# One decoder layer on one core: the RWKV inversion's blocks transposed on chip, and the S5 products rearranged

## The chip, the cores and the metric

The kernel runs on one core of one Trainium2 chip. A core has five engines with a queue each: TensorE (PE, matrix products; its weight loads are listed apart as PEld), VectorE (DVE), ScalarE (ACT), GpSimd (POOL) and SyncE (SP, which here only issues transfers). Results of matrix products lie in PSUM banks, everything else on chip in SBUF with 128 partitions; DRAM is reached by transfers (DMA). The metric is the device time of the program in microseconds (us).

## The reference

One layer of a decoder over 1024 tokens of width 1024, all in float32. Two branches, RWKV-7 and S5, are computed from one input projection, gated, merged and projected; then comes an MLP with a short convolution.

```python
h = rms_norm(x, norm_mix_pre)
p_rwkv, u_s5, gates = split(h @ w_in)               # 1792, 512 and 2048 columns

# RWKV-7, 8 heads of 64: a recurrent state S (64x64) per head
S = S * w_t + (S @ a_t) b_t^T + v_t k_t^T           # a_t = -kk, b_t = kk * a
y_t = S @ r_t
bonus = sum(r * k * r_k) * v                        # added to the normalised y

# S5, 32 groups of 16 channels with 64 complex states each
bu = einsum('gpc,blgc->blgp', b_bar, u)             # complex b_bar
s_t = a_bar * s_{t-1} + bu_t                        # complex, diagonal
y = real(einsum('gcp,blgp->blgc', c, s)) + d * u

x = x + rms_norm((g_rwkv * o_rwkv + g_s5 * o_s5) @ w_out)
x = x + rms_norm(conv_ffn(rms_norm(x)))
```

The RWKV state isn't stepped token by token: the tokens go in chunks of 64, and inside a chunk the recurrence becomes a triangular system, whose unit triangular matrices have to be inverted. The S5 recurrence is worked in steps of 8 tokens (an impulse response of 8 taps, called `kpad` and spread into the Toeplitz tile `toep`, does what lies inside a step; a scan over 128 steps does the rest), with real and imaginary parts on the two halves of the partitions. A rotation of the frame by the angle of a_bar (`cs` and `sn`, cosine and sine) leaves a scan with a real factor `ph`.

## The kernel before

**How the order comes about.** PE's order is the order in which the program is written. A function `drive()` writes it: several lanes (generators) yield how many us of PE work they have issued and how long to wait before they go on; a virtual clock `now` counts what was issued, and while all lanes wait, `background()` takes the next piece from a list of fill work. The constants T_... are these waits. So a longer wait does not stop PE: it puts more fill between two steps of a lane. The other engines' instructions are put in order by the tile framework, with priorities (`high_priority`), and wait in their queues by semaphores.

**The phases.** At first x is read and normalised. Phase 1 runs `s5_lane` and `tab_lane` over four batches of 8 groups; the fill is the input projection (`mix_in`), whose products are the three matmuls of L172 to L174 (a float32 product as three products of split high and low parts, `hh`, `hl`, `wh`, `wl`) and whose evictions are L1083 (ACT) and L1084, L1086 (DVE). Weights arrive in `wf` by SP and are split by ACT (L156) and DVE (L157). Phase 2 opens new pools of SBUF and PSUM (`rk`, `evb`, `psy`) and runs four lanes: two `prep_lane`s (pairs of heads g = 0 and 1), `chain_lane` and `out_lane`, for two halves of the tokens (th = 0 and 1). Its fill is first the gates (`gate_tiles`, evicted by ACT in L1158) and then the merge of the half that is done (`merge`, with DVE's L1203, L1249, L232). After that come the rest of the merge, the output projection and the MLP.

**S5 in a batch.** `s5_tables` makes the tables: `wT` by 8 transposes (L546) that two ACT instructions put out, with a third slice that is the negated real part; `ca` and a copy of it with halves exchanged and one negated, `cb`; `kpad` by 8 products of 16 columns each (L555), all on the same 16 output partitions, evicted by one ACT copy. `s5_batch` then makes two products B for each group (L599: `p1` and `p2`, the second with the parts exchanged), rotates them (DVE, L602 to L604), scans (L605), rotates back (L606, L607), and after a wait T_SCAN of 13 us makes three products C for each group (L612 to L614: `toep`·u, `ca`·z, `cb`·rot), which ACT evicts (L615) and SP stores in the DRAM tensor `YU` (L616).

**The RWKV inversion.** `rwkv_front` ends with the grams (L716), masked by DVE into the tile `gr` (L720). `rwkv_inv` inverts the 32x32 diagonal blocks of all heads and chunks of a half at once: 128 partitions stand for (pair of heads, block, row), and the other index pairs lie along a partition. To get there the blocks go through DRAM: 8 transfers of POOL from `gr` to `md` (L729) and one from `md` into `mt` (L777). After a wait T_MT of 8 us and the transposes of `rwkv_nat`, DVE does 30 steps of two instructions (L789, L791; the copy L784 starts them), which update the inverse `x` in place. Then `x` goes back: one transfer into `xd` (L793) and 8 into the blocks of `gr` (L798). After a wait T_INV (th 0, 43 us) or T_INV2 (th 1, 50 us) `rwkv_level` joins the 32x32 blocks to 64x64 ones, with four transposes by DVE (L812) and products of 32x32 tiles (L822).

For the bonus, `rwkv_setup` scales a block matrix of ones by r_k on DVE (L627).

Of the kernel before, what the change touches and what calls it, by code (L numbers as in the profile page):

```python
# [66 lines left out]
class Kern:  # L67
# [425 lines left out]
    def s5_tables(self, b, d):  # L493
# [37 lines left out]
        cb = self.s5p.tile([128, 8, 9, 16], F32, tag="cb", name=self.nm("cb"), bufs=2)  # L531
# [22 lines left out]
        for g in range(8):  # L554
            mm(ps[0:16, g], bb[:, g, :], ca[:, g, 0:8, :], start=g % 4 == 0, stop=True, skip_group_check=True)  # L555
        A.copy(kpad[:, :, 7:15, :], ps[0:16].rearrange("p g (j c) -> p g j c", c=16))
# [24 lines left out]
        d.update(ca=ca, cb=cb, cs=cs, sn=sn, toep=toep, wT=wT, ph=ph)  # L581
        yield 1.8, T_TRIG

    def s5_batch(self, b, d, ys):
# [4 lines left out]
        ca, cb, cs, sn, toep, wT, ph = (d[n] for n in ("ca", "cb", "cs", "sn", "toep", "wT", "ph"))  # L589
# [6 lines left out]
        p1, p2 = (self.chk().rearrange("p (g n) -> p g n", n=128) for _ in range(2))  # L596
        for p, o in ((p1, 0), (p2, 1)):
            for g in range(8):
                mm(p[:, g], wT[:, g, o:o + 2, :], u8[:, g, :], start=g % 4 == 0, stop=True, skip_group_check=True)  # L599
        r2 = self.t4(shape=(128, 8, 128))  # L600
        lead, turn = (slice(None), slice(None), slice(0, 127)), rot[:, :, 1:128]
        V.tensor_tensor(turn, p1[lead], cs[lead], ALU.mult)  # L602
        V.tensor_tensor(r2[lead], p2[lead], sn[lead], ALU.mult)
        V.tensor_tensor(turn, turn, r2[lead], ALU.add)  # L604
        V.tensor_tensor_scan(*(t.rearrange("p g n -> p (g n)") for t in (z, ph, rot)), 0.0, ALU.mult, ALU.add)  # L605
        V.tensor_tensor(rot, z, sn, ALU.mult)  # L606
        V.tensor_tensor(z, z, cs, ALU.mult)  # L607
        y8 = self.t4(shape=(128, 8, 128))
        yield 3.6, T_SCAN
        ps = self.chk().rearrange("p (g n) -> p g n", n=128)  # L610
        for g in range(8):
            mm(ps[:, g], toep[:, g], u8[:, g, :], start=g % 4 == 0, stop=False, skip_group_check=True)  # L612
            mm(ps[:, g], ca[:, g, 1:9, :], z[:, g, :], start=False, stop=False, skip_group_check=True)
            mm(ps[:, g], cb[:, g, 1:9, :], rot[:, g, :], start=False, stop=True, skip_group_check=True)  # L614
        A.copy(y8, ps)  # L615
        nc.sync.dma_start(ys.rearrange("j c g n -> (j c) g n"), y8)  # L616
        yield 5.4, 0

# [1387 lines left out]
```

## Time and profile before

| | |
|---|---|
| time, median of 3 runs | 1477.7 us (1474.89, 1477.7, 1479.7) |
| profiled execution, its time | 1475.75 us |
| its span, first to last instruction | 1474.0 us |
| mean granted clock of TensorE | 0.987 |
| ACT busy | 729.6 us (50% of the span) |
| POOL busy | 58.9 us (4%) |
| DMA | 206.26 MB, 140 GB/s mean |

The span is that of one profiled execution; its time has 1.75 us around the span. In the rows a group reads: line, engine, operation, the tile written and the tiles read, shapes, count, then busy time and mean duration, then the engine's idle time just before, and what ended it. Matmul records overlap, since they are pipelined: what a matmul costs is the distance from one start to the next, not its record's length. A float32 matmul of 128 columns shows as two records.

### The profile page before, as it was taken

What the parts mean: (1) busy time and instruction counts of PE and PEld (TensorE: products, weight loads), DVE (VectorE), ACT (ScalarE), POOL (GpSimd) and SP (SyncE); (2) the same over time, 40 slices, a digit from 0 to 9 for tenths busy, and PEclk for the clock granted to TensorE, in tenths of its full rate; (3) what the DMA queues carried; (4) which work ended last, traced back from release to release, by engine and by line L of the source; (5) the groups of instructions that cost most, each with busy time, mean ns of one, the idle gap of its engine ahead of it and who ended that gap; (6) DMA issues with size and microseconds to landing.
All of it is one profiled execution on the core that took longest, in us unless ns stands there. A gap on an engine that the chain in (4) does not pass through costs nothing. (4 is left out here: it accounts for less than half of the span.)

```text
span 1474.0 us, 24155 instructions
## 1 busy us (share of the span) xinstructions
PE 1420.3 (96%) x9284; PEld 1161.8 (79%) x9284; DVE 1072.4 (73%) x1761; ACT 729.6 (50%) x1167; POOL 58.9 (4%) x116
## 2 busy tenths in 40 slices
PE   7999999999999999899999999999999999999996
PEld 5778888788877777677788877888888887888775
DVE  8977775665425859657698798777777777697677
ACT  7677654443334653634455454444444544444441
POOL 0000000011100110100000000000000000000001
PEclk9999999999999999899999999999999999999998
DMA  6453433643511575633474543222222227934723
GB/s 219 116 194 120 134 96 88 206 123 117 171 62 63 170 238 164 187 124 108 142 223 145 192 136 112 82 86 86 86 86 86 73 71 256 341 123 140 243 75 114
DMA packets 121284, 206.26 MB, mean 140 GB/s; under 512 B 29248, under 2 KB 35520, under 8 KB 121168
## 3 DMA queue, kind: packets, MB, share of 16 engines
q1 hardware_dynamic: 113296, 182.43, 39.3%
q0 software_dynamic: 6144, 19.99, 4.0%
q10 hardware_dynamic: 1728, 2.29, 0.4%
q8 instruction: 73, 1.20, 0.3%
q14 instruction: 43, 0.35, 0.1%
HBM read 150.14 MB, written 52.43 MB: 137 GB/s over the span
## 5 line engine op out<-in xcount | busy, mean ns | idle before, releaser
L172 PE MATMUL gm<-hh,wh 128*128 128x512 f32 x672 | 276.4, 411 | 9.4 <-DVE ev L1203 4.1
L173 PE MATMUL gm<-hl,wh 128*128 128x512 f32 x672 | 264.8, 394 | 0.1
L174 PE MATMUL gm<-hh,wl 128*128 128x512 f32 x672 | 264.5, 394 | 0.0
L156 ACT CAST wh<-wf 128x512 fp32r<-128x512 f32 x171 | 105.7, 619 | 167.4 <-PE gm L173 99.5
L157 DVE TENSOR_TENSOR wl<-wf,wh 128x512 fp32r<-128x512 f32 x171 | 117.3, 688 | 75.7 <-ACT wh L156 75.1
L172 PEld LDWEIGHTS gm<-hh,wh 128*128 128x128 f32 x672 | 127.5, 190 | 42.1 <-issue 6.0
L174 PEld LDWEIGHTS gm<-hh,wl 128*128 128x128 f32 x672 | 127.6, 190 | 28.0
L173 PEld LDWEIGHTS gm<-hl,wh 128*128 128x128 f32 x672 | 127.8, 190 | 24.7 <-issue 1.0
L1626 PE MATMUL d<-xl,wh 128*128 128x512 f32 x308 | 120.2, 390 | 2.8 <-DVE xl L227 2.8
L1625 PE MATMUL d<-xh,wh 128*128 128x512 f32 x308 | 120.1, 390 | 2.1 <-ACT xh L226 2.1
L1627 PE MATMUL d<-xh,wl 128*128 128x512 f32 x308 | 119.9, 389 | 0.0
L1451 PE MATMUL rp<-t,h 128*128 128x512 f32 x216 | 84.4, 391 | 1.9 <-ACT p L1465 1.9
L1453 PE MATMUL rp<-t,l 128*128 128x512 f32 x216 | 84.2, 390 | 0.5 <-DVE l L227 0.5
L1452 PE MATMUL rp<-t,h 128*128 128x512 f32 x216 | 84.1, 389 | 0.0
L1626 PEld LDWEIGHTS d<-xl,wh 128*128 128x128 f32 x308 | 57.8, 188 | 15.6 <-DVE xl L227 3.9
L1625 PEld LDWEIGHTS d<-xh,wh 128*128 128x128 f32 x308 | 57.8, 188 | 14.5 <-ACT xh L226 2.4
L1627 PEld LDWEIGHTS d<-xh,wl 128*128 128x128 f32 x308 | 57.8, 188 | 12.0
L226 ACT CAST h<-r 128x1024 fp32r<-128x1024 f32 x34 | 35.8, 1054 | 61.1 <-PE rp L1452 29.6
L227 DVE TENSOR_TENSOR l<-r,h 128x1024 fp32r<-128x1024 f32 x34 | 41.7, 1225 | 29.3 <-ACT h L226 27.7
L1472 DVE SCALAR_TENSOR_TENSOR y<-zv,vecs,y 128x1023 f32<-128x1023 f32 (+1 forms) x36 | 46.1, 1281 | 8.5 <-ACT y L1470 8.5
L1451 PEld LDWEIGHTS rp<-t,h 128*128 128x128 f32 x216 | 40.5, 188 | 11.3 <-ACT p L1465 2.7
L1465 ACT COPY p<-rp 128x512 f32<-128x512 f32 x54 | 31.0, 574 | 36.6 <-PE rp L1453 36.6
(459 smaller groups left out, 3163.7 us busy)
## 6 DMA issues: line engine op xcount, KB each, us to landing
r<-in_w_up_dram SPq DMA_DIRECT2D x36, 512.0 KB, 3.7
wf<-in_w_in_dram SPq DMA_DIRECT2D x62, 256.0 KB, 3.1
st<-in_w_down_dram SPq DMA_DIRECT2D x55, 256.0 KB, 4.1
st<-ACT SPq DMA_DIRECT2D x44, 256.0 KB, 4.3
wf<-in_w_up_dram SPq DMA_DIRECT2D x36, 256.0 KB, 2.9
ACT<-y POOLq DMA_DIRECT2D x18, 512.0 KB, 2.9
GT<-ev SPq DMA_DIRECT2D x32, 256.0 KB, 2.5
wf<-in_w_br_dram SPq DMA_DIRECT2D x32, 256.0 KB, 2.9
```

The source lines that it names most:

```text
L156: nc.scalar.copy(h[:, :n], f[:, :n])
L157: nc.vector.tensor_tensor(l[:, :n], f[:, :n], h[:, :n].bitcast(F32), ALU.subtract)
L172: mm(ps, a, xh[k], start=k == 0, stop=False)
L173: mm(ps, a, xl[k], start=False, stop=False)
L174: mm(ps, b, xh[k], start=False, stop=k == n - 1)
L1451: mm(ps, wh[:, c], xh, start=first and k == 0, stop=False, skip_group_check=True)
L1452: mm(ps, wh[:, c], xl, start=False, stop=False, skip_group_check=True)
L1453: mm(ps, wl[:, c], xh, start=False, stop=k == 3, skip_group_check=True)
L1472: V.scalar_tensor_tensor(y[:, lag:], z[:, 0:1024 - lag], self.vec(nme, i), y[:, lag:], ALU.mult, ALU.add)
L1625: mm(ps, wh[:, c], xh[:, x], start=start, stop=False, skip_group_check=True)
L1626: mm(ps, wh[:, c], xl[:, x], start=False, stop=False, skip_group_check=True)
L1627: mm(ps, wl[:, c], xh[:, x], start=False, stop=stop, skip_group_check=True)
```

## The change

- **S5, B.** Only `p1` is multiplied. The second product is replaced by two ACT instructions that copy the halves of `p1`, exchanged and one negated, into `r2`; DVE's product with `sn` is then made in place. `wT` holds 128 columns for each group and is evicted by one ACT copy.
- **S5, C.** `cb` is gone with its two ACT copies. The rotated back part is joined on DVE: ACT exchanges the halves of `z` into `rot`, DVE multiplies with `sn` and `cs` and adds, and one product with `ca` is left beside the one with `toep`.
- **S5, impulse response.** The 8 products of `kpad` go to four groups of 32 output partitions (q = 0, 32, 64, 96, two products each), evicted by four ACT copies in place of one.
- **Inversion.** `md`, `xd` and their transfers (8 + 1 + 1 + 8 of POOL in each half) are gone. A new function `diagonal` copies the blocks between `gr` and the inversion's tile, 8 copies each way, in turn on DVE and ACT; DVE transposes the whole tile in 32x32 blocks before and after the steps. The tile is made by a copy of 128x1024 and a memset of the diagonal. The 30 steps have q columns in place of q + 1. The tie of the first copy to `rwkv_nat` is gone.
- **Waits.** T_SCAN 13 to 24, T_MT 8 to 3, T_INV 43 to 34, T_INV2 50 to 46.
- **Pools and r_k.** The eviction pool `evb` is opened ahead of `rk`; the r_k products are POOL's.

The diff, cut:

```diff
@@ s5_tables
-        cb = self.s5p.tile([128, 8, 9, 16], F32, tag="cb", name=self.nm("cb"), bufs=2)
-        A.copy(cb[HALF[0], :, 1:9, :], ca[HALF[1], :, 1:9, :])
-        A.mul(cb[HALF[1], :, 1:9, :], ca[HALF[0], :, 1:9, :], -1.0)
-        wT = self.s5p.tile([128, 8, 3, 64], F32, tag="wT", name=self.nm("wT"))
+        wT = self.s5p.tile([128, 8, 128], F32, tag="wT", name=self.nm("wT"))
-        A.copy(wT[:, :, 0:2, :], ps.rearrange("p g (a n) -> p g a n", n=64))
-        A.mul(wT[:, :, 2, :], ps[:, :, 0:64], -1.0)
-        yield 1.0, 0
+        A.copy(wT, ps)
+        yield 0.9, 0
         for g in range(8):
-            mm(ps[0:16, g], bb[:, g, :], ca[:, g, 0:8, :], start=g % 4 == 0, stop=True, skip_group_check=True)
-        A.copy(kpad[:, :, 7:15, :], ps[0:16].rearrange("p g (j c) -> p g j c", c=16))
+            q = 32 * (g % 4)
+            mm(ps[q:q + 16, g // 4 * 4], bb[:, g, :], ca[:, g, 0:8, :], start=True, stop=True, skip_group_check=True)
+        for q in range(4):
+            A.copy(kpad[:, q::4, 7:15, :], ps[32 * q:32 * q + 16, 0::4].rearrange("p g (j c) -> p g j c", c=16))
@@ s5_batch
-        p1, p2 = (self.chk().rearrange("p (g n) -> p g n", n=128) for _ in range(2))
-        for p, o in ((p1, 0), (p2, 1)):
-            for g in range(8):
-                mm(p[:, g], wT[:, g, o:o + 2, :], u8[:, g, :], start=g % 4 == 0, stop=True, skip_group_check=True)
+        p1 = self.chk().rearrange("p (g n) -> p g n", n=128)
+        for g in range(8):
+            mm(p1[:, g], wT[:, g], u8[:, g, :], start=g % 4 == 0, stop=True, skip_group_check=True)
+        A.copy(r2[HALF[0]], p1[HALF[1]])
+        A.mul(r2[HALF[1]], p1[HALF[0]], -1.0)
         V.tensor_tensor(turn, p1[lead], cs[lead], ALU.mult)
-        V.tensor_tensor(r2[lead], p2[lead], sn[lead], ALU.mult)
+        V.tensor_tensor(r2, r2, sn, ALU.mult)
...
-        V.tensor_tensor(rot, z, sn, ALU.mult)
+        A.mul(rot[HALF[0]], z[HALF[1]], -1.0)
+        A.copy(rot[HALF[1]], z[HALF[0]])
         V.tensor_tensor(z, z, cs, ALU.mult)
+        V.tensor_tensor(rot, rot, sn, ALU.mult)
+        V.tensor_tensor(z, z, rot, ALU.add)
-        yield 3.6, T_SCAN
+        yield 1.8, T_SCAN
...
-            mm(ps[:, g], ca[:, g, 1:9, :], z[:, g, :], start=False, stop=False, skip_group_check=True)
-            mm(ps[:, g], cb[:, g, 1:9, :], rot[:, g, :], start=False, stop=True, skip_group_check=True)
+            mm(ps[:, g], ca[:, g, 1:9, :], z[:, g, :], start=False, stop=True, skip_group_check=True)
...
-        yield 5.4, 0
+        yield 3.6, 0
@@ rwkv_setup
-            nc.vector.tensor_scalar(self.rkb[:, p], self.cst("ones_bd"), self.vec("r_k", p), None, ALU.mult)
+            nc.gpsimd.tensor_tensor(self.rkb[:, p], self.cst("ones_bd"), self.vec("r_k", p).to_broadcast([128, 128]), ALU.mult)
@@ rwkv_front
-                for blk in range(2):
-                    for h in range(2):
-                        q = 64 * h + 32 * blk
-                        nc.gpsimd.dma_start(d["md"][blk].rearrange("(e h) q t -> h q e t", h=2)[h],
-                                            d["gr"][q:q + 32, :, :, h, 32 * blk:32 * blk + 32].rearrange("p u c t -> p (u c) t"))
@@ rwkv_inv
+    def diagonal(self, ds, m, back):
+        m = m.rearrange("p (e h t) -> p e h t", h=2, t=32)
+        n = 0
+        for g, d in enumerate(ds):
+            for blk in range(2):
+                for h in range(2):
+                    o, q = 64 * h + 32 * blk, 32 * (2 * g + blk)
+                    x = d["gr"][o:o + 32, :, :, h, 32 * blk:32 * blk + 32].rearrange("p u c t -> p (u c) t")
+                    y = m[q:q + 32, :, h]
+                    (self.nc.scalar.copy if n % 2 else self.nc.vector.tensor_copy)(*((x, y) if back else (y, x)))
+                    n += 1
...
-            nc.gpsimd.memset(x, 0.0)
-            nc.gpsimd.memset(x[:, 0:1024:33], 1.0)
-            nc.gpsimd.dma_start(mt, self.md[th].rearrange("g b e q t -> (g b e) (q t)"))
+            self.diagonal(ds, x, False)
+            V.transpose(mt.rearrange("p (q t) -> p t q", t=32), x.rearrange("p (e t) -> p t e", t=32))
+            V.tensor_copy(x, mt)
+            V.memset(x[:, 0:1024:33], 1.0)
...
-            self.nc.scalar.copy(x2[:, 0, 1:2], tie[:, 0, 0:1])
-            V.tensor_copy(x2[:, 0, 1:32], mt[:, 0, 1:32])
             for q in range(1, 31):
-                n, m = q + 1, 31 - q
+                m = 31 - q
...
-            nc.gpsimd.dma_start(xds.rearrange("g b e s t -> (g b e) (s t)"), x)
...
+            V.transpose(mt.rearrange("p (e t) -> p t e", t=32), x.rearrange("p (q t) -> p t q", t=32))
+            self.diagonal(ds, mt, True)
@@ front_half and the constants
-        with tc.tile_pool(name="rk", bufs=1) as self.rk, tc.tile_pool(name="evb", bufs=NEV) as self.evp, \
+        with tc.tile_pool(name="evb", bufs=NEV) as self.evp, tc.tile_pool(name="rk", bufs=1) as self.rk, \
-T_US, T_TAB0, T_TAB, T_TRIG, T_SCAN = 5.0, 44.0, 20.0, 12.0, 13.0
+T_US, T_TAB0, T_TAB, T_TRIG, T_SCAN = 5.0, 44.0, 20.0, 12.0, 24.0
-T_KN, T_BK, T_GR, T_NF, T_MT, T_INV, T_LV, T_CH = 7.0, 4.0, 4.0, 5.0, 8.0, 43.0, 1.0, 0.8
-T_LN, T_LE, T_INV2 = 32.0, 16.0, 50.0
+T_KN, T_BK, T_GR, T_NF, T_MT, T_INV, T_LV, T_CH = 7.0, 4.0, 4.0, 5.0, 3.0, 34.0, 1.0, 0.8
+T_LN, T_LE, T_INV2 = 32.0, 16.0, 46.0
```

What this does to the order, at three places. In a row stand the line, the operation, the tile written and the tiles read (numbers tell buffers and uses apart), the shape, and xN for N alike.

**PE, end of phase 1.** The last rows of the C product of batch 3 (`chk_2705`, before; `t_552` is `rot`) and the fill behind it, before:

```order
L612 MATMUL chk_2705<-u_3_180,t_538_2449 128x128
L613 MATMUL chk_2705<-t_551_2562,ca_2283 128x128
L614 MATMUL chk_2705<-t_552_2563,cb_2285 128x128
L172 MATMUL gm_2749<-hh_561,wh_2737 128x512
L173 MATMUL gm_2749<-hl_562,wh_2737 128x512
L174 MATMUL gm_2749<-hh_561,wl_2738 128x512
L172 MATMUL gm_2749<-hh_578,wh_2737 128x512
L173 MATMUL gm_2749<-hl_579,wh_2737 128x512
```

and now:

```order
L613 MATMUL chk_2838<-u_3_180,t_541_2489 128x128
L614 MATMUL chk_2838<-t_556_2615,ca_2304 128x128
L172 MATMUL gm_2822<-hh_669,wh_2816 128x512
L173 MATMUL gm_2822<-hl_670,wh_2816 128x512
L174 MATMUL gm_2822<-hh_669,wl_2817 128x512
L172 MATMUL gm_2822<-hh_686,wh_2816 128x512
L173 MATMUL gm_2822<-hl_687,wh_2816 128x512
L174 MATMUL gm_2822<-hh_686,wl_2817 128x512
L172 MATMUL gm_2822<-hh_726,wh_2816 128x512
L173 MATMUL gm_2822<-hl_727,wh_2816 128x512
L174 MATMUL gm_2822<-hh_726,wl_2817 128x512
L172 MATMUL gm_2913<-hh_731,wh_2810 128x512
```

Two products stand for each group where three stood, and behind the product now stand the last nine matmuls of the gate tile `gm_2822` and then the next gate tile, where a whole tile of the input projection, `gm_2749`, stood before.

**DVE, start of the second inversion (th 1).** `gr_5254` and `gr_5246` are the masked grams of heads pair 1, `mt` the inversion's tile. Before:

```order
L720 TENSOR_TENSOR gr_5254<-cz_5699,csts 128x4x128
L736 TENSOR_TENSOR ld_5355<-rp_5718,ld_5523 128x512
L736 TENSOR_TENSOR ld_5358<-rp_5720,ld_5526 128x512
L227 TENSOR_TENSOR hl_5971<-ld_5958,hh_5970 128x512
L227 TENSOR_TENSOR hl_5975<-ld_5960,hh_5974 128x512
L157 TENSOR_TENSOR wl_5982<-wf_5983,wh_5981 128x512
L157 TENSOR_TENSOR wl_6021<-wf_6022,wh_6020 128x512
L157 TENSOR_TENSOR wl_6060<-wf_6061,wh_6059 128x512
L227 TENSOR_TENSOR hl_6006<-hh_6001,hh_6005 128x512
L227 TENSOR_TENSOR hl_6014<-hh_6009,hh_6013 128x512
L784 COPY mt_5758<-mt_5758 128x31
L789 TENSOR_TENSOR tm_5845<-mt_5758 128x60
```

and now:

```order
L719 TENSOR_TENSOR gr_5246<-cz_5675,csts 128x4x128
L773 COPY mt_5730<-gr_5246 32x16x32 x2
L227 TENSOR_TENSOR hl_5767<-ld_5756,hh_5766 128x512
L784 STREAM_TRANSPOSE mt_5730<-mt_5730 128x32x32
L227 TENSOR_TENSOR hl_5771<-ld_5758,hh_5770 128x512
L157 TENSOR_TENSOR wl_5961<-wf_5962,wh_5960 128x512
L785 COPY mt_5730<-mt_5730 128x1024
L227 TENSOR_TENSOR hl_5775<-ld_5760,hh_5774 128x512
L795 TENSOR_TENSOR tm_5835<-mt_5730 128x30
L786 MEMSET mt_5730 128x32
L730 TENSOR_TENSOR ld_5331<-rp_5694,ld_5527 128x512
L797 TENSOR_TENSOR mt_5730<-mt_5730,tm_5835 128x30
```

The steps began behind nine other instructions (among them the two of L736); now the block copies, the transpose and the copy of the whole tile (L773, L784, L785) stand close behind the grams, with the splits of the fill between them, and L730 (which was L736) comes after the first step.

**DVE, end of the second inversion.** Before, up to the last transposes of `rwkv_level` (L812):

```order
L1203 SCALAR_TENSOR_TENSOR ev_6457<-ev_6457,gm_6465 128x512
L227 TENSOR_TENSOR hl_6454<-ld_6450,hh_6453 128x512
L157 TENSOR_TENSOR wl_6900<-wf_6901,wh_6899 128x512
L1249 TENSOR_TENSOR ev_6457<-ev_6457,hl_6203 128x512
L812 STREAM_TRANSPOSE ld_6487<-gr_4905 32x512 x2
L232 SCALAR_TENSOR_TENSOR hl_6502<-ev_6457,hh_6501 128x512
L1203 SCALAR_TENSOR_TENSOR ev_6513<-ev_6513,gm_6521 128x512
L227 TENSOR_TENSOR hl_6510<-ld_6506,hh_6509 128x512
L1249 TENSOR_TENSOR ev_6513<-ev_6513,hl_6252 128x512
L812 STREAM_TRANSPOSE ld_6488<-gr_5254 32x512 x2
```

and now, from the last step on (the first L812 row follows 21 rows further on, among the same kinds of rows):

```order
L795 TENSOR_TENSOR tm_5922<-mt_5730 128x30
L797 TENSOR_TENSOR mt_5730<-mt_5730,tm_5922 128x30
L798 STREAM_TRANSPOSE mt_5730<-mt_5730 128x32x32
L157 TENSOR_TENSOR wl_6365<-wf_6366,wh_6364 128x512
L773 COPY gr_4897<-mt_5730 32x16x32 x2
L773 COPY gr_5246<-mt_5730 32x16x32 x2
L1203 SCALAR_TENSOR_TENSOR ev_6238<-ev_6238,gm_6246 128x512
L1203 SCALAR_TENSOR_TENSOR ev_6265<-ev_6265,gm_6273 128x512
L157 TENSOR_TENSOR wl_6400<-wf_6401,wh_6399 128x512
L1249 TENSOR_TENSOR ev_6238<-ev_6238,hl_5778 128x512
L1249 TENSOR_TENSOR ev_6265<-ev_6265,hl_5957 128x512
L232 SCALAR_TENSOR_TENSOR hl_6262<-ev_6238,hh_6261 128x512
```

The transpose L798 and the copies L773 stand on DVE directly behind the last step, where POOL issued nine transfers.

More of the change, by code (lines that the diff above doesn't have):

```diff
@@ L579, in s5_tables @@
         G.memset(ph[:, :, 0:1], 0.0)
-        d.update(ca=ca, cb=cb, cs=cs, sn=sn, toep=toep, wT=wT, ph=ph)
+        d.update(ca=ca, cs=cs, sn=sn, toep=toep, wT=wT, ph=ph)
         yield 1.8, T_TRIG
@@ L588, in s5_batch @@
         mm = nc.tensor.matmul
-        ca, cb, cs, sn, toep, wT, ph = (d[n] for n in ("ca", "cb", "cs", "sn", "toep", "wT", "ph"))
+        ca, cs, sn, toep, wT, ph = (d[n] for n in ("ca", "cs", "sn", "toep", "wT", "ph"))
         u8 = self.u8[b]
@@ L1855, in front_half @@
             self.fronts, self.masked, self.preps, self.chains, self.chunks, self.outs, self.z = 0, 0, 0, 0, 0, 0, {}
-            self.md = [self.dram.tile([2, 2, 32, 32, 32], F32, name=f"md{th}") for th in range(2)]
             self.pts = [self.tg("pt", 2, (128, 8, 4)) for th in range(2)]
```

22 lines of the change are left out of this document (7 added, 15 removed).

## The prediction

> **What bounds the kernel now.** I read the page's first parts (which engine is full, and what ends last), then the table of stretches, then what PE waits for.
>
> ```profile
> span 1474.0 us, 24155 instructions
> PE 1420.3 (96%) x9284; PEld 1161.8 (79%) x9284; DVE 1072.4 (73%) x1761; ACT 729.6 (50%) x1167; POOL 58.9 (4%) x116
> PE   7999999999999999899999999999999999999996
> ...
> 120.00:262.00 142.00, 142.00 (x823) 123.27 (x822) 97.05 (x125) 80.77 (x142) 3.30 (x10) 1.00 0.35 106
> 490.00:640.00 150.00, 136.28 (x1243) 108.73 (x1241) 107.26 (x213) 79.39 (x156) 14.96 (x24) 0.94 0.61 179
> ```
>
> PE is busy for 96% of the span. The last two rows are stretches (length, then busy PE, PEld, DVE, ACT, POOL, PE's clock): from 120 to 262 us, where the S5 batches run, PE doesn't idle at all, with DVE at 97.05/142 = 68%. There each us of PE work taken away is a us of the span, so long as DVE and ACT keep up. From 490 to 640 us, around the second inversion, PE idles 13.7 us and its clock drops to 0.94. There PE is not the only bound. Its waits in that stretch, and the one wait at the end of phase 1:
>
> ```profile
> PE gm L172 <- ACT wh L156: 1.8, 1, 1.8
> ...
> PE gm L172 <- DVE ev L1203: 4.1, 2, 3.1
> PE gm L172 <- ACT ev L1158: 2.6, 2, 1.5
> PE rp L702 <- ACT ld L937: 2.2, 1, 2.2
> PE rp L822 <- ACT hh L231: 2.0, 1, 2.0
> ```
>
> The merge's evictions on DVE and splits on ACT hold PE up, not POOL's transfers: those are waited for through the DVE and ACT rows behind them.
>
> **The change: S5's products.** PE's timeline of one batch (start, length):
>
> ```profile
> 166.49 3.73 PE L599 MATMUL chk<-u,wT 128*128 128x128 f32 x32
> 169.98 0.48 PE L172 MATMUL gm<-hh,wh 128*128 128x512 f32 x1
> ...
> 182.61 1.92 PE L555 MATMUL chk<-ca,sml 128*16 128x128 f32 x16
> 184.46 0.50 PE L172 MATMUL gm<-hh,wh 128*128 128x512 f32 x1
> ...
> 185.26 0.38 PE L612 MATMUL chk<-u,t 128*128 128x128 f32 x2
> 185.48 0.39 PE L613 MATMUL chk<-t,ca 128*128 128x128 f32 x2
> 185.70 0.39 PE L614 MATMUL chk<-t,cb 128*128 128x128 f32 x2
> 185.92 0.39 PE L612 MATMUL chk<-u,t 128*128 128x128 f32 x2
> ```
>
> B's 16 products take 169.98 − 166.49 = 3.49 us; half go: 1.745. A group's three C products take 185.92 − 185.26 = 0.66 us, one 0.22; 8 go: 1.76. In four batches 4 × (1.745 + 1.76) = **14.0 us**. `kpad` takes 184.46 − 182.61 = 1.85 us in a batch for 16 records, 116 ns each. Products that lie beside each other in the array are in the trace only as the grams:
>
> ```profile
> L716 PE MATMUL cz<-ar,bk 64*64 64x128 f32 x512 | 16.3, 273 | 0.2 <-DVE gr L720 0.2
> ```
>
> 16.3 us for 512 records is 32 ns a record. At that price `kpad` takes 0.51 and saves 1.34 a batch, 5.4 in all; if the four groups don't overlap it saves nothing. I take 0.6 us a batch, near the grams' row: 4 × 1.25 = **5.0 us**. In all PE's work falls by 19.0 us.
>
> The Trainium skill, "TensorE: Matmul & The Clock Gate", Part 3, says that column tiles reached 2.38 times with three groups. By that `kpad` would take 1.85/2.38 = 0.78 us, an estimate, and save 4.3 us in place of 5.0; no run here has shown column groups.
>
> **Does the S5 chain stay hidden?** Between B and C now run:
>
> ```profile
> L602 DVE TENSOR_TENSOR t<-chk,t x4: 1205/1217/1218, 136.0 to 239.9; 128x1016 f32<-128x1016 f32 x4
> L605 DVE TENSOR_TENSOR_SCAN t<-t,t x4: 2284/2284/2292, 141.3 to 244.3; 128x1024 f32<-128x1024 f32 x4
> L615 ACT COPY t<-chk x4: 1017/1018/1020, 155.1 to 260.7; 128x1024 f32<-128x1024 f32 x4
> ```
>
> (The three numbers are ns, least, median, most.) Two ACT copies (2 × 1.02; 1024 elements lie along a partition, as in L615), two DVE products (1.22 each), the scan (2.28), two ACT copies beside a DVE product (2.04), a product and a sum (2.44): 11.2 us. On PE stand 96 matmuls of 128x512 between B and C in place of 54; at 0.227 us (nine take 2.04 in rows further down) that is over 21.8 us, and the chain has some 10 us to spare for other rows in the queues of DVE and ACT. A batch keeps its length on PE, some 35 us: more fill stands in it for the 4.75 us that go, and the gain shows where that fill is missing later. In it DVE gains a sum of 1.22 us, ACT four copies of 1.02 less the two of `cb`, the second of `wT` (half as long) and a little for `kpad`, below 2 us; both stay under 75%. I count this at 0. Without that cover each us of chain beyond 21.8 costs PE one, four times. The r_k products lie on POOL (4% busy) and are first read behind the first grams: 0. The pools' order moves addresses only; what it changes lies within the bounds of the boundary.
>
> **The boundary of the phases.**
>
> ```profile
> 266.26 0.69 ACT L1083 ACTIVATE ev<-gm,mu 128x512 f32<-128x512 f32 x1 [4.56 <-PE gm L174]
> 266.98 0.75 DVE L1084 SCALAR_TENSOR_TENSOR ev<-gm,vecs,ev 128x511 f32<-128x511 f32 x1 [0.42 <-ACT ev L1083]
> 267.64 0.15 DVE L1086 COPY last<-gm 128x1 f32<-128x1 f32 x1
> ...
> 267.94 0.61 PE L172 MATMUL gm<-hh,wh 128*128 128x512 f32 x1 [1.85 <-ACT wh L156]
> 268.35 0.63 PE L173 MATMUL gm<-hl,wh 128*128 128x512 f32 x1
> ...
> 271.66 0.40 PE L172 MATMUL gm<-hh,wh 128*128 128x512 f32 x1
> 271.89 0.39 PE L173 MATMUL gm<-hl,wh 128*128 128x512 f32 x1
> ...
> L1178 ACT ACT_TABLE_LOAD  x1: 1283/1283/1283, 535.6 to 535.6; - x1
> ```
>
> PE waits 1.85 us, then goes at half speed: nine matmuls take 271.66 − 267.94 = 3.72 us, where at 0.227 (271.89 − 271.66 is 0.23) nine take 2.04. The price is 1.85 + 1.68 = 3.5 us. The wait is put down to a split of weights, but what ends just ahead of it is the eviction of the last tile of the old PSUM pool, on ACT (266.26) and then on DVE (to 267.79): the first product in the new pool needs its bank. Now that tile is a gate tile, with nine matmuls behind C (2.0 us). ACT first copies `y8` (1.02), loads a function table (1.28) and then evicts (0.69, as L1083): some 3.3 us behind C, so PE waits about 1.3. The gain is 0.5, or 2.2 if the half-speed stretch goes too; between 0 and 3.5 I take **1.0**, nearer to the first, since a wait stays. The next weights' load waits for `y8`'s store on SP's queue as before, and is wanted 24 matmuls (5.5 us) later than the new pool.
>
> The same page of the Trainium skill, in "Why this matters for your kernels", advises against PE gaps above some 3 us; by it no half speed would follow a wait of 1.3 us, and the gain would be 2.2. The trace disagrees: 1.85 us were enough.
>
> **The inversions.** Stretches around the second one, with rows of DVE and of the transfers that go (median us to landing):
>
> ```profile
> 531.50:614.70 83.20, 72.77 (x423) 58.20 (x423) 65.44 (x138) 47.93 (x87) 10.09 (x16) 0.97 0.69 199
> 531.50:548.00 16.50, 15.02 (x77) 12.39 (x76) 6.09 (x11) 13.53 (x24) 4.32 (x7) 1.00 0.86 262
> 548.00:592.30 44.30, 42.43 (x186) 34.11 (x185) 43.15 (x102) 19.58 (x37) 0.00 (x0) 1.00 0.53 160
> 592.30:614.70 22.40, 15.32 (x164) 11.71 (x164) 16.20 (x27) 14.82 (x27) 5.77 (x9) 0.88 0.89 229
> ...
> L789 DVE TENSOR_TENSOR tm<-mt x60: 202/364/427, 351.0 to 590.2; 128x60 f32<-128x60 f32 x4, 128x87 f32<-128x87 f32 x4, 128x112 f32<-128x112 f32 x4, 128x135 f32<-128x135 f32 x4
> L812 DVE STREAM_TRANSPOSE ld<-gr x8: 692/701/703, 395.5 to 613.9; 32x512 f32<-32x512 f32 x8
> md<-gr POOLq DMA_DIRECT2D x16, 64.0 KB, 4.6
> gr<-xd POOLq DMA_DIRECT2D x16, 64.0 KB, 3.8
> ```
>
> While the steps run DVE is full (43.15 of 44.3 us). Before and after them, while the blocks go through DRAM, it isn't. So the round trips leave, but the new work lands on the full engine. For each half: four copies in and four out on DVE (32x16x32, 512 elements along a partition; half of 2 × a 1024 copy, 0.47 with overhead, by L615: 3.8 us), two transposes of 1024 (L812 does 512 in 0.70; without its fixed part about 1.2: 2.5 us), the 1024 copy and memset (0.8 to 1.3), less 1.0 for 930 elements fewer in the steps (L789: 0.20 us for 31, 0.43 for 240, about 1 ns each) and 0.2 for L784: **+6.3 us of DVE**. PE's rows in that place hold 263 matmuls of 128x512 where 302 stood: 39 × 0.227 = 8.9 us of fill go elsewhere, and no longer cover DVE. Summing the rows from the last gram to the last L822, PE's work falls from 74.2 to 65.4 us, DVE's rises from 67.0 to 73.4. Before, the place took 86.7 us, 12.5 above PE's work. Now DVE starts some 6 us behind the last gram (its inputs come by ACT) and is then full: about 80 us, 14.6 above PE's work. That is a loss of 2, up to 5 where ACT's half of the copies comes late (ACT's order puts loads' activations ahead); I take **−3**. For the unknown prices: if DVE's copies take as a two-input row does, 0.69, it is 1.8 us worse; if ACT's half hides and the waits shorten, up to 4.5 better (80 becomes 73.4 plus 2).
>
> At the first inversion the fill hides all of it: with the round trips gone it ends some 17 us ahead of the level's first row on PE. Cost 0; if that cover goes, at most the +6.3.
>
> **Sum.** 1475.75 − 19.0 − 1.0 + 3 = 1458.75 us for an execution like the profiled one. The median of the runs lies 1.95 above it: **1460.5 us**.
>
> **Rivals.**
> - *Better*: the half-speed stretch at the boundary goes too (2.2 to 3.5), and the second inversion, without round trips of 4.6 and 3.8 us and more, is no worse or 4.5 better. 1477.7 − 19.0 − 2.2 − (0 to 4.5): 1452 to 1456.5. With 3.5 at the boundary and `kpad` at 5.4 it is 1450, and the runs spread by 2.8 below their median. For it: 7.1 us of PE idle and a clock of 0.88 from 592.3 on. Against: those waits are for merge rows on DVE and ACT, which stay.
> - *DVE's queue takes more*: block copies, transposes and evictions of the merge queue up, PE runs dry more often, and each gap adds half speed. A loss of 8 to 15 in place of 3: 1465.5 to 1472.5. For it: DVE's 43.15 of 44.3; against: round trips gone.
> - *`kpad` doesn't do what it should*: column groups one after another, 5.0 back: 1465.5.
> - *Within 0.3%* (1473.3 to 1482.1, about what a measurement can tell from no change): a loss of 16 to 24 at the second inversion, the new DVE rows at about three times their price.
> - *Slower*: the same rows (3.8 + 2.5 + 1.1 = 7.4 us by their nearest rows) cost four times that, since copies and transposes step 32 or more elements through memory: 22 us more, with DVE full, all of it PE's: above 1482. It decides at four times. Against: L789's operands step through memory too, and 240 elements take 0.43 us.
>
> **Chances.** Forecast 0.47 (1457 to 1464), better 0.17, DVE's queue 0.13, `kpad` 0.05: faster 0.82. Within 0.3% 0.10, slower 0.08. The range leaves out the slower case and most of the one within: 1449 to 1473.
>
> **What would show it.** From 120 us to the end of phase 1 PE stays without idle, and phase 1 ends some 6 us later than before (the last batch has 108 matmuls between B and C, where 60 were), with more fill done; `kpad`'s row takes 0.5 to 0.8 us. At the boundary a wait of about 1.3 us ends on ACT L1158. From the last gram to L822 some 80 us, DVE full, no POOL rows. It is wrong if C waits for DVE in phase 1, if the block copies take well above 0.5 us, or if PE idles by over 8 us more between 500 and 620.

## The result and the profile after

| | before | changed |
|---|---|---|
| median of the runs | 1476.3 us (4 runs) | 1461.5 us (1458.3 to 1462.8, 4 runs) |
| ratio | | 0.9884, 95% interval 0.9861 to 0.9907 |
| span of the profiled execution | 1474.0 us | 1459.5 us |

The page of the changed kernel and its two stretches around the S5 batches and the second inversion (length, then busy time of PE, PEld, DVE, ACT, POOL, PE's clock, the DMA share and GB/s):

```profile
span 1459.5 us, 23887 instructions
PE 1402.2 (96%) x9156; PEld 1142.9 (78%) x9156; DVE 1087.5 (75%) x1783; ACT 746.7 (51%) x1197; POOL 34.9 (2%) x80
...
120.00:270.00 150.00, 148.95 (x805) 126.04 (x804) 106.11 (x139) 97.56 (x167) 3.32 (x11) 1.00 0.38 117
490.00:640.00 150.00, 131.87 (x1494) 102.79 (x1493) 107.35 (x207) 81.46 (x154) 1.08 (x2) 0.94 0.52 160
```

PE's busy time fell by 18.1 us, the span by 14.5. Up to the boundary of the phases PE still doesn't idle (the 1.05 us missing in the first stretch are the boundary); around the second inversion it idles 18.1 us in place of 13.7 (from 500 to 620 us 15.7 in place of 12.6, well below the 8 more that the prediction named as a sign of being wrong). Its waits there:

```profile
PE gm L172 <- DVE hl L1203: 4.6, 2, 3.9
PE gm L172 <- DVE ev L1203: 3.1, 2, 2.2
PE rp L822 <- DVE ld L812: 3.0, 1, 3.0
PE cz L822 <- ACT hh L231: 2.2, 1, 2.2
PE rp L701 <- ACT ld L937: 2.0, 1, 2.0
PE rp L756 <- DVE ld L730: 1.7, 1, 1.7
```

The new instructions themselves (ns, least, median and most, first and last start), and the packed `kpad` as a group:

```profile
L773 DVE COPY mt<-gr x8: 404/417/420, 307.2 to 517.3; 32x512 f32<-32x512 f32 x8
L773 ACT COPY mt<-gr x8: 616/617/620, 307.3 to 517.5; 32x512 f32<-32x512 f32 x8
L784 DVE STREAM_TRANSPOSE mt<-mt x2: 2207/2232/2256, 335.3 to 518.3; 128x1024 f32<-128x1024 f32 x2
L785 DVE COPY mt<-mt x2: 679/712/745, 337.9 to 521.6; 128x1024 f32<-128x1024 f32 x2
...
L551 PE MATMUL chk<-ca,sml 128*16 128x128 f32 x64 | 2.5, 275 | 0.0
```

`kpad` takes 2.5 us for 64 records, 39 ns each or 0.62 us a batch: the column groups do overlap. The prediction took 0.47 us for a block copy on DVE and about 1.25 for each of these transposes: the copies are a little cheaper (0.42), the transposes 1.8 times as dear.

For the rest, the program is cut at five places that both kernels have, and each stretch's length is compared with the kernel before. What the change in PE's work explains is taken off (0.227 us for each 128x512 matmul more or less between the two places in PE's order, and the S5 products): the last column is what the stretch costs beside its work.

| stretch of the changed kernel | length, us | against before | by PE's work | beside it |
|---|---|---|---|---|
| start to the end of the last C product | 265.8 | +5.4 | +6.2 | −0.8 |
| to the first grams (the boundary lies in it) | 28.3 | −4.9 | −3.4 | −1.5 |
| to the first level (L822) | 90.6 | −14.2 | −14.3 | +0.1 |
| to the last gram of the second half | 125.6 | −1.5 | 0 | −1.5 |
| to the last L822 of the second level | 89.1 | −1.9 | −8.8 | **+6.9** |
| to the end | 860.1 | +2.6 | +1.4 | +1.3 |
| sum | 1459.5 | −14.5 | −19.0 | +4.5 |

### The profile page after: what moved, and what is told of

Same layout as the page of the kernel before. It is cut to its first block, busy times and chain, and to the rows that moved or that the text cites. A ratio compares the mean times of both kernels' runs of the same rounds, so it can differ in the third digit from the quotient of the medians.

```text
span 1459.5 us, 23887 instructions
## 1 busy us (share of the span) xinstructions
PE 1402.2 (96%) x9156; PEld 1142.9 (78%) x9156; DVE 1087.5 (75%) x1783; ACT 746.7 (51%) x1197; POOL 34.9 (2%) x80
## 5 line engine op out<-in xcount | busy, mean ns | idle before, releaser
L172 PE MATMUL gm<-hh,wh 128*128 128x512 f32 x672 | 276.2, 411 | 9.1 <-DVE hl L1203 4.6
L172 PEld LDWEIGHTS gm<-hh,wh 128*128 128x128 f32 x672 | 127.5, 190 | 41.5 <-DVE hl L1203 5.7
L1626 PEld LDWEIGHTS d<-xl,wh 128*128 128x128 f32 x308 | 58.2, 189 | 15.5 <-DVE xl L227 3.4
L226 ACT CAST h<-r 128x1024 fp32r<-128x1024 f32 x34 | 35.8, 1054 | 61.1 <-PE rp L1452 29.6
L227 DVE TENSOR_TENSOR l<-r,h 128x1024 fp32r<-128x1024 f32 x34 | 41.6, 1225 | 29.2 <-ACT h L226 27.7
```

Source lines behind the costliest of these rows:

```text
L172: mm(ps, a, xh[k], start=k == 0, stop=False)
L227: (eng or self.nc.vector).tensor_tensor(lo, x, hi.bitcast(F32), ALU.subtract)
L1626: mm(ps, wh[:, c], xl[:, x], start=False, stop=False, skip_group_check=True)
```

## The experiments

Twelve kernels were run. Each ratio is against executions of the kernel before that were taken along with that kernel; their medians lay between 1476.3 and 1478.5 us, so that 2 us between the medians of two experiments mean little. The word **lead** is used for one number: how many 128x512 matmuls PE has in its order ahead of the last gram of the second half, more than the kernel before has there. It says how far the fill is ahead of the lanes. The changed kernel has 33: 111 more by the end of phase 1, since the lanes' waits are filled up where S5's products left, 15 fewer to the first grams, 63 fewer to the first level.

### Each part alone

s5_only is the kernel before with the diff's hunks in `s5_tables` and `s5_batch` (lead 93), inv_only the one with those in `rwkv_tiles`, `rwkv_front`, `diagonal` and `rwkv_inv` (lead −63), each with its own constants; pools and r_k are as before in both.

```diff
@@ s5_only
-T_US, T_TAB0, T_TAB, T_TRIG, T_SCAN = 5.0, 44.0, 20.0, 12.0, 13.0
+T_US, T_TAB0, T_TAB, T_TRIG, T_SCAN = 5.0, 44.0, 20.0, 12.0, 24.0
@@ inv_only
-T_KN, T_BK, T_GR, T_NF, T_MT, T_INV, T_LV, T_CH = 7.0, 4.0, 4.0, 5.0, 8.0, 43.0, 1.0, 0.8
-T_LN, T_LE, T_INV2 = 32.0, 16.0, 50.0
+T_KN, T_BK, T_GR, T_NF, T_MT, T_INV, T_LV, T_CH = 7.0, 4.0, 4.0, 5.0, 3.0, 34.0, 1.0, 0.8
+T_LN, T_LE, T_INV2 = 32.0, 16.0, 46.0
```

> The kernel before with the S5 part alone (B once, one C product, packed kpad, T_SCAN 24); inversion, T_MT, T_INV, T_INV2, pools and r_k as before. Theory Q (the second inversion's new work on DVE and ACT costs the changed kernel about 7 us in the place from the last gram to the last L822 row): that loss is absent here, so 1476.3 - 19.0 (PE's work) - 2.5 (boundary of the phases) = about 1455, ratio 0.985 to 0.987. Rival R (the loss comes from the S5 part, which lets the fill run ahead, so that merge rows meet the inversion): the place around the second inversion loses 7 us here too, about 1461, ratio 0.990.

> The kernel before with the inversion part alone (blocks copied and transposed on chip, T_MT 3, T_INV 34, T_INV2 46); S5, T_SCAN, pools and r_k as before. PE's work is that of before. Theory Q: about 7 us lost from the last gram to the last L822 row, nothing elsewhere: 1481 to 1484, ratio 1.003 to 1.005. Rival R: no loss, or a gain of 1 to 2 us since the transfers are gone: 1474 to 1477, ratio 0.999 to 1.000.

Measured: s5_only 1491.8 us, ratio 1.0077 (1.0057 to 1.0098), inv_only 1493.7, ratio 1.0089 (1.0067 to 1.0111). Both theories fell: each part alone is **slower** by nearly 1%, and together they are faster. s5_only shows two reasons. PE's wait, what ACT waited for, and SP's issues in its trace, as three pieces of the timelines:

```profile
541.58 0.80 PE L172 MATMUL gm<-hh,wh 128*128 128x512 f32 x1 [13.44 <-ACT hh L226]
...
540.91 1.27 ACT L226 CAST hh<-ld 128x512 fp32r<-128x512 f32 x2 [6.50 <-DMA ld<-YR]
...
532.43 1.37 SPq L950 DMA_DIRECT2D YR<-ld  x2
534.43 0.32 SPq L944 DMA_DIRECT2D ld<-bv  x1
535.16 0.32 SPq L944 DMA_DIRECT2D ld<-TG  x1
536.72 0.85 SPq L1210 DMA_DIRECT2D ld<-YR  x2
```

The fill has come to the merge of the first half, whose input `YR` the `out_lane` is only just storing: PE, which keeps its order, stands for 13.4 us. That stretch (first level to last gram) costs 25.7 us beside its work. The second reason is at the boundary:

```profile
265.91 1.02 ACT L615 COPY t<-chk 128x1024 f32<-128x1024 f32 x1 [6.23 <-PE chk L614]
269.85 1.28 ACT L1158 ACT_TABLE_LOAD   x1 [2.92 <-DMA YU<-t]
271.14 0.69 ACT L1158 ACTIVATE ev<-gm,hb_b_gate 128x512 f32<-128x512 f32 x1
...
271.88 0.50 PE L172 MATMUL gm<-hh,wh 128*128 128x512 f32 x1 [3.96 <-ACT ev L1158]
```

In this kernel, with the pools in the old order and r_k on DVE, the gate's eviction waits until `y8` is stored in `YU`, and half speed follows PE's wait (matmuls 0.43 us apart). In inv_only the inversion's own place costs 5.1 us less than before beside its work; it loses 19.4 us behind it, where 102 more matmuls of fill stand, those that the shorter waits no longer took. PE waits there once for 6.6 us (L172, for ACT's split L231) and five times for 6.1 us in all (L879, for DVE's L904).

### Waits alone: the lead

Three kernels that change only waits, one with the inversion part at the old waits, two with the changed kernel and a shorter T_INV:

```diff
@@ inv_oldT, from inv_only; lead 0
-T_KN, T_BK, T_GR, T_NF, T_MT, T_INV, T_LV, T_CH = 7.0, 4.0, 4.0, 5.0, 3.0, 34.0, 1.0, 0.8
-T_LN, T_LE, T_INV2 = 32.0, 16.0, 46.0
+T_KN, T_BK, T_GR, T_NF, T_MT, T_INV, T_LV, T_CH = 7.0, 4.0, 4.0, 5.0, 8.0, 43.0, 1.0, 0.8
+T_LN, T_LE, T_INV2 = 32.0, 16.0, 50.0
@@ inv30, from the changed kernel; lead 18 (inv24 with 24.0; lead -9)
-T_KN, T_BK, T_GR, T_NF, T_MT, T_INV, T_LV, T_CH = 7.0, 4.0, 4.0, 5.0, 3.0, 34.0, 1.0, 0.8
+T_KN, T_BK, T_GR, T_NF, T_MT, T_INV, T_LV, T_CH = 7.0, 4.0, 4.0, 5.0, 3.0, 30.5, 1.0, 0.8
```

> The kernel before with the on-chip inversion and all waits of before (T_MT 8, T_INV 43, T_INV2 50, T_SCAN 13), so that each fill matmul stands where it stood. Theory F (the losses are set by how far the fill is ahead of the lanes, not by the inversion's own rows): nothing is lost, the inversions only end earlier: 1474 to 1479, ratio 0.997 to 1.001, and the place from the last gram to the last L822 row within 2 us of before. Theory Q (DVE's new rows cost 7 us in that place): 1483 to 1486, ratio 1.004 to 1.006.

> The changed kernel with T_INV 30.5 in place of 34: 15 fill matmuls (3.4 us) less before the first level, so that at the second grams the fill is 18 matmuls of 128x512 ahead of the kernel before in place of 33. Theory F: the place around the second inversion loses 3 to 5 us in place of 6.9, the end gives back 0 to 2: 1458 to 1461. Theory Q: 6.9 as before, 1461 within 2 us.

> The changed kernel with T_INV 24: the fill is 9 matmuls behind the kernel before at the second grams. Theory F: the place around the second inversion loses nothing (the part with the inversion alone, 63 behind, gained 5 there); the end, where that kernel lost 19 us, loses 2 to 5: 1456 to 1462. Theory Q: 1461 within 2 us, with 6.9 lost in the place. If the first inversion is no longer ready when PE wants it (some 10 us less cover, of about 17), PE waits before the first L822 row.

A fourth, s5_undone, puts the hunks of `s5_tables` and `s5_batch` back into the changed kernel and sets T_SCAN so that the fill stands as in it:

```diff
-T_US, T_TAB0, T_TAB, T_TRIG, T_SCAN = 5.0, 44.0, 20.0, 12.0, 24.0
+T_US, T_TAB0, T_TAB, T_TRIG, T_SCAN = 5.0, 44.0, 20.0, 12.0, 22.0
```

> The changed kernel with the S5 products of before (two B products, three C products, kpad on one group of partitions) and T_SCAN 22, at which the fill stands at every place from the first grams on as in the changed kernel. PE has 19.0 us more work. Theory F (what a part costs besides its work is set by where the fill stands): 1461.5 + 19.0, and 0 to 2 at the boundary: 1480 to 1483, with every stretch behind the first grams within 2 us of the changed kernel's. If the inversion part loses by its own rows, as inv_only's 1493.7 could be read: 1490 or more.

Costs beside PE's work, in us against the kernel before, in the three last stretches:

| kernel | lead | first level to last gram | to the last L822 | to the end | median, ratio |
|---|---|---|---|---|---|
| inv_only | −63 | +1.2 | −5.1 | +19.4 | 1493.7, 1.0089 |
| inv24 | −9 | +1.0 | −2.0 | +11.8 | 1464.7, 0.9908 (0.9872 to 0.9944) |
| inv_oldT | 0 | −1.1 | +0.9 | +5.4 | 1481.9, 1.0017 (0.9997 to 1.0038) |
| inv30 | 18 | +4.0 | −0.2 | +7.4 | 1468.7, 0.9934 (0.9908 to 0.9960) |
| changed kernel | 33 | −1.5 | +6.9 | +1.3 | 1461.5, 0.9884 |
| s5_undone | 33 | −0.8 | +4.2 | +3.6 | 1481.2, 1.0021 (1.0008 to 1.0034) |
| scan13 (further down) | 57 | +1.5 | +15.0 | +2.2 | 1495.4, 1.0104 |
| s5_only | 93 | +25.7 | −0.7 | +8.8 | 1491.8, 1.0077 |

(The last stretch holds the down projection, which took 214 to 217 us in these kernels with the same rows; 2 us there mean nothing. In the place of the second inversion the three kernels with one order there, the changed one, s5_undone and kpad_flat below, cost 6.9, 4.2 and 4.2, so that 3 us are within what one profile can be off.) inv_oldT has all the new instructions of the inversion and costs 0.9 us in the place where the changed kernel costs 6.9. The windows from the last gram to the last L822 (columns as above) of the kernel before, the changed one, inv_oldT, inv24 and scan13:

```profile
525.48:616.49 91.01, 80.58 (x509) 64.26 (x505) 70.76 (x145) 49.90 (x91) 10.09 (x16) 0.96 0.69 202
...
510.28:599.37 89.09, 73.95 (x469) 58.66 (x466) 77.15 (x154) 52.98 (x94) 1.08 (x2) 0.92 0.60 183
...
524.51:616.46 91.95, 81.72 (x509) 64.55 (x505) 78.01 (x155) 53.88 (x96) 1.08 (x2) 0.95 0.63 186
...
503.57:583.78 80.21, 72.20 (x469) 57.34 (x465) 66.14 (x135) 45.02 (x83) 1.08 (x2) 0.95 0.57 167
...
540.74:637.91 97.17, 79.65 (x470) 61.06 (x466) 79.37 (x158) 54.75 (x96) 1.08 (x2) 0.89 0.54 165
```

In inv_oldT DVE is as busy as in the changed kernel (78.0 and 77.2 us), but there 39 more matmuls cover it. Its time lies between the two forecasts: the place behaved as theory F says, but the end cost 5.4 us, which neither theory had. As the lead falls the loss leaves the place (inv30, inv24) and comes back at the end, in inv30 also ahead of the place (+4.0); at lead 57 the place costs 15.0. So the expected gains of inv30 and inv24 didn't come: inv30 is slower than the changed kernel, inv24 can't be told from it.

One thing goes along with the lead, and these runs don't part it from the lead: DVE's busy time in the place. With the same inversion and the same 39 matmuls fewer it is 59.3 us in inv_only, 66.1 in inv24, 70.9 in inv30, 77.2 in the changed kernel and 79.4 in scan13, and the place grows in the same order (77.2, 80.2, 82.0, 89.1 and 97.2 us long), since a larger lead brings more of DVE's rows for the merge into it. In s5_only, with the inversion of before, the place costs nothing at lead 93: there the stretch ahead of it had already lost 25.7. s5_undone landed in its expected range, 19.7 us above the changed kernel for 19.0 us of work, though two stretches differ by 2.7 and 2.3 us.

### DVE's share, and the order of its queue

Both from the changed kernel:

```diff
@@ diag_act
-                    (self.nc.scalar.copy if n % 2 else self.nc.vector.tensor_copy)(*((x, y) if back else (y, x)))
+                    self.nc.scalar.copy(*((x, y) if back else (y, x)))
@@ lvprio, rwkv_level
+            with self.tc.high_priority(HPW):
...
                     V.transpose(xz[lo[h]].rearrange("p u c t -> p (u c) t"),
```

> The changed kernel with all 16 block copies of each half on ACT (DVE's 8 copies a half leave it, 3.3 us; ACT does 16 of 0.62). If DVE's fullness around the second inversion sets the loss there, it falls by about 3 us: 1458, and DVE's busy time in that place falls from 77.0 to about 73.7. If late inputs through ACT set it (ACT's queue holds splits that DVE waits for), it grows by 2 to 5 us: 1463 to 1466.

> The changed kernel with the four transposes L812 of each level at the priority of the weights' splits, so that DVE does them ahead of the merge's rows. If the order of DVE's queue holds the second level up (2.95 us of PE's wait on the last L812, behind rows that wait for ACT and a transfer), those 3 us go: 1458 to 1459. If the wait only moves to the merge's rows: 1461 within 2 us.

diag_act: 1468.0 us, ratio 0.9918 (0.9896 to 0.9940). DVE's busy time in the place fell as forecast, from 77.2 to 74.0 us, the cost beside the work stayed (7.1), and 2.3 and 3.4 us came in the two stretches ahead of it. The time lies above both forecasts. DVE's share of the copies doesn't seem to hold the place up; but the 3 us that were forecast are no more than what one profile can be off, so that this run weighs against DVE's load and doesn't rule it out. lvprio: 1460.8, ratio 0.9875 (0.9841 to 0.9909); the 2.95 us wait on L812 went and the place cost 2.5 instead of 6.9, but the chain behind it took 3.7 us longer (61.1 against 57.4). It can't be told from the changed kernel.

The longest wait of the place in the changed kernel runs through three queues, on PE, DVE and ACT:

```profile
533.21 0.50 PE L172 MATMUL gm<-hh,wh 128*128 128x512 f32 x1 [3.90 <-DVE hl L1203]
...
531.61 0.69 DVE L227 TENSOR_TENSOR hl<-hh,hh 128x512 fp32r<-128x512 f32 x1 [1.24 <-ACT hh L226]
532.22 0.34 DVE L795 TENSOR_TENSOR tm<-mt 128x184 f32<-128x184 f32 x1
532.48 0.68 DVE L1203 SCALAR_TENSOR_TENSOR hl<-ev,gm 128x512 f32<-128x512 f32 x1
...
529.41 1.13 ACT L1178 ACTIVATE hh<-ld 128x512 f32<-128x512 f32 x1 [1.31 <-DMA ld<-YU]
530.57 0.36 ACT L761 COPY V<-rp 64x256 f32<-64x256 f32 x1
530.96 0.62 ACT L226 CAST hh<-hh 128x512 fp32r<-128x512 f32 x1
```

PE waits for an eviction (L1203), which stands on DVE behind a split (L227) that waits for ACT, which waited for a load of `YU`. DVE idles there for 1.24 us: what is late is the merge's input, and an engine that keeps its order passes it on. That chain isn't shown to be what the lead costs: in inv30, inv24 and inv_oldT PE waits nearly as long once in the place (3.26, 3.36 and 3.34 us), for the eviction of a gate (L1158) instead. All PE's waits in the place above 0.4 us come to 15.0 us in the changed kernel and to 9.5, 7.7 and 10.1 in those three (9.9 before).

### The S5 chain

The changed kernel with T_SCAN back at 13:

```diff
-T_US, T_TAB0, T_TAB, T_TRIG, T_SCAN = 5.0, 44.0, 20.0, 12.0, 24.0
+T_US, T_TAB0, T_TAB, T_TRIG, T_SCAN = 5.0, 44.0, 20.0, 12.0, 13.0
```

> The changed kernel with T_SCAN back at 13: 57 to 60 matmuls of 128x512 between B and C, 12.9 to 13.6 us, in place of 96 to 108. If the S5 chain takes the 11.2 us of my sum, C finds z ready and the time stays at 1461 within 3 us. If the chain is as long as the trace of the changed kernel shows (21.4, 21.3, 17.3 and 15.9 us from B's end to the last sum), PE waits about 8, 8, 4 and 2 us at C, each wait with half speed behind it: 1485 to 1495.

Measured 1495.4 us, ratio 1.0104 (1.0078 to 1.0130): the chain is long. Not all of the 33.9 us above the changed kernel are its price: 20.7 lie up to the last C product, beside PE's work (PE's four waits at C, 15.5 us, and half speed behind two of them), and 8.1 around the second inversion, where this kernel has the lead 57. Waits of scan13 from 120 to 290 us, and in the changed kernel's timeline B, the last sum and the first C of a batch:

```profile
PE chk L614 <- DVE t L608: 15.5, 4, 7.3
...
164.78 1.95 PE L595 MATMUL chk<-u,wT 128*128 128x128 f32 x16
186.63 1.22 DVE L608 TENSOR_TENSOR t<-t,t 128x1024 f32<-128x1024 f32 x1
190.02 0.38 PE L613 MATMUL chk<-u,t 128*128 128x128 f32 x2
```

From the end of B's records (166.73) to the sum's (187.85) are 21.1 us, and 2.2 are left to the first C.

### `kpad`, the layout of the copies, the transfers

All three from the changed kernel; dma_newT puts back the hunks of `rwkv_tiles`, `rwkv_front` and `rwkv_inv` (the inversion through DRAM) and keeps every new wait.

```diff
@@ kpad_flat
-            q = 32 * (g % 4)
-            mm(ps[q:q + 16, g // 4 * 4], bb[:, g, :], ca[:, g, 0:8, :], start=True, stop=True, skip_group_check=True)
-        for q in range(4):
-            A.copy(kpad[:, q::4, 7:15, :], ps[32 * q:32 * q + 16, 0::4].rearrange("p g (j c) -> p g j c", c=16))
+            mm(ps[0:16, g], bb[:, g, :], ca[:, g, 0:8, :], start=g % 4 == 0, stop=True, skip_group_check=True)
+        A.copy(kpad[:, :, 7:15, :], ps[0:16].rearrange("p g (j c) -> p g j c", c=16))
@@ contig
-        m = m.rearrange("p (e h t) -> p e h t", h=2, t=32)
+        m = m.rearrange("p (t e h) -> p e h t", h=2, t=32)
-            V.transpose(mt.rearrange("p (q t) -> p t q", t=32), x.rearrange("p (e t) -> p t e", t=32))
+            V.transpose(mt.rearrange("p (q t) -> p t q", t=32), x.rearrange("p (t e) -> p t e", t=32))
-            V.transpose(mt.rearrange("p (e t) -> p t e", t=32), x.rearrange("p (q t) -> p t q", t=32))
+            V.transpose(mt.rearrange("p (t e) -> p t e", t=32), x.rearrange("p (q t) -> p t q", t=32))
```

> The changed kernel with the kpad products on one group of 16 output partitions and one eviction, as before; the fill stands where it stood. If the four column groups overlap and PE bounds phase 1, PE's 1.85 in place of 0.62 us a batch shows in full: 1461.5 + 4.9 = 1466.4. If they don't bound anything: 1461.5 within 2 us.

> The changed kernel with the block copies laid out so that each of the two transposes of 128x1024 reads or writes one side in order (the other side still steps 32 elements). If the step makes a transpose take 2.22 us where two of 512 in order take 1.4, L784 and L798 fall to between 1.2 and 1.8 us, and the copies rise by 0.2 at most; the time falls by 0 to 2 us: 1459.5 to 1461.5. If it is the length and not the step, they stay at 2.2.

> The changed kernel with the inversion through DRAM of before and its own new waits (T_MT 3, T_INV 34, T_INV2 46). In the kernel before, the first level came some 64 us behind the end of the first grams, with its transposes waiting for nothing but their place; the changed kernel has 52.6 us of rows there. If moving the blocks on chip is what lets the waits be shorter: PE waits 8 to 12 us at the first L822 row with half speed behind it, and 0 to 6 us at the second: 1472 to 1482. If the transfers were hidden anyway: 1461.5 within 2 us.

kpad_flat: 1468.3 us, ratio 0.9931 (0.9910 to 0.9953), 6.8 above the changed kernel's median; the three batches that lie between the first B and the last C got 3.84 us longer, 1.28 each, as their work says. contig: 1470.5, ratio 0.9942 (0.9921 to 0.9962), where a small gain was expected:

```profile
L784 DVE STREAM_TRANSPOSE mt<-mt x2: 2024/2072/2120, 336.6 to 522.4; 128x1024 f32<-128x1024 f32 x2
L773 DVE COPY mt<-gr x8: 585/634/640, 306.7 to 520.6; 32x512 f32<-32x512 f32 x8
L773 ACT COPY mt<-gr x8: 1077/1138/1152, 306.8 to 521.2; 32x512 f32<-32x512 f32 x8
```

The transposes hardly got shorter, and copies that step through the tile take 0.63 and 1.14 us in place of 0.42 and 0.62; the way to the first level costs 3.3 us more than in the changed kernel and the second inversion 10.8 beside its work, in place of 6.9. The copies rose by 0.2 us on DVE and 0.5 on ACT, where 0.2 at most was expected. dma_newT: 1470.9, ratio 0.9948 (0.9929 to 0.9968). PE waited 1.03 us at the first level, not 8 to 12: the transfers came nearly in time for the shorter wait there. It is 9.4 us slower than the changed kernel: beside the work 1.5 us more up to the first level, 5.9 up to the last gram and 2.3 around the second inversion. That much moving the blocks on chip is worth at these waits; what takes the 5.9 us was not looked into.

## Why the prediction held, and where it didn't

The forecast was 1460.5 us; 1461.5 were measured. (The prediction's last sum, 1458.75 + 1.95, gives 1460.7; 1460.5 adds 1.75.) Step by step:

- **S5's products, 14.0 + 5.0 us: right**, in size too. s5_undone gives 19.7 us for the whole, kpad's row 0.62 us a batch against 0.6. The Trainium skill's 2.38 times ("TensorE: Matmul & The Clock Gate", Part 3, three groups) would have given 0.78; four groups came to 1.85/0.62 = 3.0 times.
- **The S5 chain at 0: right for the time, wrong in its working.** The prediction counted 11.2 us with 10 to spare. The chain took some 21, 21, 17 and 16 us, since rows of other work stand between its own in the queues of DVE and ACT and, in the first batch, a table it reads is late (DVE waits 2.7 us for it). Only 2 us of cover were left in the first two batches, so that this term stayed at nothing by a margin that the prediction didn't know; scan13 shows the price without it. A sum of durations is a lower bound of a chain, not its length.
- **The boundary, −1.0: too small.** PE's wait was 1.05 us, near the forecast 1.3, but no half speed followed, so the wait and its tail fell by 2.5 us (from 1.85 + 1.68 to 1.05). Here the same page of the Trainium skill ("Why this matters for your kernels") gave the better number, 2.2, though half speed did follow a wait of 2.17 us elsewhere in the changed kernel (571.14), below the 3 us that it names. The stretch as a whole won 1.5. "The pools' order moves addresses only" was too light: in s5_only, which has the old order and r_k on DVE, the eviction waits 2.92 us for a store, and the stretch costs 3.7 us more than in the changed kernel. The two edits weren't run apart; that the wait is for the store is what its row says.
- **The first inversion at 0: right** (+0.1), and inv24 with 9.5 us less cover paid only 0.3.
- **The second inversion, −3 (2 to 5): the mis-sized term.** It cost 6.9 us in the profiled execution; the two other kernels with this order cost 4.2 there, inside the forecast's 2 to 5, so how far it was off isn't certain. DVE's extra work was right: 6.4 forecast, 6.4 measured (77.15 − 70.76), with dearer transposes and cheaper copies. The length was not: 86.7 us were counted for the place before and some 80 forecast, 91.0 and 89.1 were measured. In the forecast DVE starts 6 us behind the last gram and is then full; in the changed kernel it idles for 11.9 of the 89.1 us, in many short waits. The reason given, that the new rows land on a full DVE while less fill covers it, is not refuted: with the fill of before around them the same rows cost 0.9 (inv_oldT). What it leaves out is that the same rows cost nothing with that fill gone too, when the lead is smaller (−0.2 at 18, −2.0 at −9). So the size of the loss goes by where the fill stands. Whether it works through more merge rows on DVE or through late inputs of these rows stays open: DVE's load falls with the lead as well, and diag_act speaks against the load only as far as one profile can tell 3 us.
- **Rest.** −0.8, −1.5 and +1.3 us in other stretches were not forecast and nearly cancel. Beside the work, 2 us of loss were forecast in all and 4.5 measured; for an execution like the profiled one that is 1461.3 where 1458.75 were forecast. The rest of the nearness is luck: the prediction set the median 1.75 us above that execution, and it came 0.2 above it.

So the main term, PE's 19.0 us, was right, and the 3.9 us by which the second inversion was dearer were hidden by gains elsewhere and by the median. It helped that the forecast was worked out from the order of the whole changed kernel: as a sum of two parts it would have failed, since s5_only is 13 us and inv_only 15 us above their runs of before, and the whole is 15 below. What stays open, beside the way in which the lead costs time, is the end: inv_only's waits there are shown above, inv24's longest is 5.1 us (L172, for DVE's L139), but inv30 has none above 1.1 us up to 900 us and still loses 7.4. Open is also why the merge's loads of `YU` land when they do.

## What to carry to other kernels

Where fill work in a fixed order covers the waits of other lanes, PE time saved in one stretch isn't won there: it moves the fill ahead, and the fill can then reach work whose inputs aren't ready (13.4 us in s5_only). After such a change, compare for each lane how far the fill stands ahead of it, and set the waits again; and test parts of a change only with the fill at the same place. A chain's length comes from the queues that it runs in, not from the sum of its instructions.

## What the runs showed of the hardware that was not expected

- A transpose of 128x1024 in 32x32 blocks takes 2.2 us on DVE where 32x512 takes 0.70; with one side in order it still takes 2.07 to 2.10.
- A block copy of 512 elements along 32 partitions takes 0.42 us on DVE and 0.62 on ACT; with one side stepping 32 elements in place of whole rows, 0.63 and 1.14.
- PE's half speed doesn't follow from a wait's length alone: a wait of 1.85 us (kernel before) and one of 2.17 (changed kernel, 571.14) were followed by some eight matmuls at 0.43 us, one of 2.03 us (495.21) and one of 1.05 were not.
